# An ordinary first pair in gate and up, and a new end of the down projection, in a layer with two feed-forward halves

## The chip, the cores and the metric

The kernel runs on one core of a Trainium2 chip. The metric is the device time of one execution in microseconds (us). Times in this document are of that kind; TensorE does the matrix products, VectorE and ScalarE the elementwise work, GpSimd a third share of it, and the transfers of this kernel are issued by SyncE.

## The reference

One layer over x of 1024 x 1024 float32, in three residual parts: a feed-forward half, a token mixer, and a second feed-forward half.

```
def swiglu_ffn(x, w_gu, w_down):
    gu = x @ w_gu                       # 1024 x 5632
    g, u = jnp.split(gu, 2, axis=-1)    # gate and up, 2816 each
    return (jax.nn.silu(g) * u) @ w_down
...
x = layer_norm(ALPHA * x + 0.5 * swiglu_ffn(x, ffn1_w_gu, ffn1_w_down), ln1_g, ln1_b)
x = layer_norm(ALPHA * x + hybrid_mixer(x, ...), ln2_g, ln2_b)
x = layer_norm(ALPHA * x + 0.5 * swiglu_ffn(x, ffn2_w_gu, ffn2_w_down), ln3_g, ln3_b)
```

The mixer is gated linear attention and a sparse attention beside each other, with one projection before and one after.

## The kernel before

x is cut into eight blocks of 128 rows; each block has two halves of 512 columns. The feature axis of 2816 has 22 tiles of 128, taken in 11 pairs (`g`). Every matrix product is done in split precision: each operand is split into a high and a low part (`split`, ScalarE L92 for the high part, VectorE L93 for the low one), and a product of two tiles is three matmuls: high by high, high by low, low by high.

Gate and up are done with a scheme of seven block products in place of eight (Strassen's in Winograd's form). x as a whole is one 2 x 2 matrix of quarters: row blocks 0 to 3 or 4 to 7 times left or right half. The quarters "11" and "21" are the two column halves of blocks 0 to 3, "12" and "22" those of blocks 4 to 7; "T1" to "T4" are sums of quarters, and the products use 11, 21, 22 and the four sums. Each of them must first be turned: `turn_in` transposes one half of one block on TensorE in four 128 x 128 pieces into a bank of PSUM (L246, tile `tp`, two banks), and ScalarE and VectorE split it into the tiles `b_h`, `b_l` and the like. The weights' sums are made on GpSimd (L275 to L278) for every pair, for gate and for up (`quad_weights`).

`quad` does the seven products of one pair, of gate or of up. A product is four steps of three matmuls of 128x512 (L300 to L302). In the first pair, the list `self.fill` holds the turns that are still missing, with the sums that they need (L1066 and L1071 on VectorE, L1068 and L1080 on GpSimd); after each step one item of it is popped, so the turns stand between the first products' steps. TensorE takes its instructions in the order in which they were written there (`in_order`). A turn that waits for its x block thus holds the products behind it. In the first half x is loaded from memory at the kernel's start; in the second, blocks 6 and 7 still come out of LayerNorm 2 (L205 to L220) as the first pair begins.

The down projection (`down`) does its seven products `m` = 0 to 6 over 11 steps `i`, each for four row blocks. `prepare` loads a pair of tiles (L410, L411) and splits it into `whid` and `wlod`, in a ring of six; `add` does the matmuls (L420). After a product VectorE adds it into the accumulators and into `u`. In the last product the last five `i` are held back (`ends`), so that its four blocks end one after the other, and each goes through LayerNorm at once (`after_block`). In the first half, `after_all` already turns the blocks 0 to 3 for the mixer between the steps of that last product (`split_T`, TensorE L180, ScalarE L181, VectorE L182). A LayerNorm is two statistics (L205), an aggregate (L207), a small addition (L209), a power on GpSimd (L193), and then either ScalarE L218, GpSimd L219 and VectorE L220, or, for the very last block, VectorE L213 and L214 alone.

Where the order is not written by hand, a planner with costs and due times sets it, in the mixer above all.

Of the kernel before, what the change touches and what calls it, by code (L numbers as in the profile page):

```python
# [111 lines left out]
class Block:  # L112
# [87 lines left out]
    def layer_norm(self, t, g_bc, b_bc, scale=1.0, last=False):  # L200

        nc = self.nc
        st = self.small.tile([P, 2, 6], F32, tag="st", name=self.uid("st"))
        for c in range(2):
            nc.vector.bn_stats(st[:, c, :], t[:, c * 512 : (c + 1) * 512])  # L205
# [6 lines left out]
        if last:  # L212
            nc.vector.scalar_tensor_tensor(t, t, mv[:, 0:1], g_bc, ALU.subtract, ALU.mult)  # L213
            nc.vector.scalar_tensor_tensor(t, t, rs, b_bc, ALU.mult, ALU.add)  # L214
        else:
# [4 lines left out]
            nc.vector.tensor_add(t, t, b_bc)  # L220

# [27 lines left out]
    def feed(self, b, t):  # L249

        if b >= NB // 2:
            self.turn_in(t[:, 512:], b % 4, "22")
        else:
            self.turn_in(t[:, 0:512], b % 4, "11")
            self.turn_in(t[:, 512:], b % 4, "21")

    def quad_raw(self, w_gu, c0):

        r = []
        for k in range(2):  # L260
# [24 lines left out]

    def quad(self, a, weights, ps, cp):
# [6 lines left out]
        def product(left, right):  # L293
            pool, tag, n = ((ps, "y", 2), (ps, "z", 2), (self.ps_pj, "pj", 2))[self.turn % 3]
            self.turn += 1
            bank = pool.tile([P, HT], F32, tag=tag, name=self.uid("pq"), bufs=n)
            wh, wl = a[left]
            xh, xl = self.sums[right]
            for k in range(4):
                nc.tensor.matmul(bank, wh[:, k, :], xh[:, k, :], start=(k == 0), stop=False)  # L300
                nc.tensor.matmul(bank, wh[:, k, :], xl[:, k, :], start=False, stop=False)  # L301
                nc.tensor.matmul(bank, wl[:, k, :], xh[:, k, :], start=False, stop=(k == 3))  # L302
                if self.fill:
                    self.fill.pop(0)()
            return bank

        def tile(name):
            i = self.made_c % sum(n for _, n in cp)
            self.made_c += 1
            pool, n = cp[0] if i < cp[0][1] else cp[1]  # L310
            return pool.tile([P, HT], F32, tag="c", name=self.uid(name), bufs=n)
# [21 lines left out]
    def gate_up(self, w_gu, first, ps, cp, h_dram, w_down, t_dram):  # L333
# [5 lines left out]
        for g in range(NF // 2):  # L339
            if g == 0:  # L340
                both = [self.quad(*w, ps, cp) for w in first]
                for q in both:
                    next(q)
            prods = []
            for i, c0 in enumerate((2 * g * P, FF + 2 * g * P)):
                if g == 0:
                    prods.append(next(both[i]))
                else:
                    a = {}
                    w = self.quad_weights(self.quad_raw(w_gu, c0), a)  # L350
                    next(w)
                    prods.append(list(self.quad(a, w, ps, cp))[-1])
                if i == 0:
                    for t in prods[0]:
                        nc.scalar.activation(t, t, AF.Silu)  # L355
            if g == 0:
                yield
            for t, q in zip(*prods):
                V.tensor_mul(t, t, q)
            (a11, a21, a12, a22), (s1, s2, s4, _) = prods  # L360
            V.tensor_add(s1, a21, a22)
            V.tensor_sub(s2, s1, a11)
            V.tensor_sub(a21, a11, a21)
            V.tensor_sub(s4, a12, s2)
            left = {"A11": a11, "A12": a12, "A22": a22, "S1": s1, "S2": s2, "S3": a21, "S4": s4}
            for m, (name, _) in enumerate(self.DOWN):
                nc.sync.dma_start(h_dram[g][m], left[name])
            if g:
                self.down_sums(w_down, t_dram, g - 1)
        self.down_sums(w_down, t_dram, NF // 2 - 1)  # L370
# [19 lines left out]
    def down(self, w_down, h_dram, t_dram, ps, load, after_block, after_all=None, ordered=None):  # L390
# [33 lines left out]
        ends = range(ng - 5, ng)  # L424
        done = list(range(4))
        acc = None
        for m in range(last + 1):
# [4 lines left out]
            for i in range(ng if m < last else ends[0]):  # L432
# [7 lines left out]
                if m == last and after_all and i >= 2:  # L440
# [3 lines left out]
            for r in range(4):  # L444
# [9 lines left out]
                elif m in (4, 5):  # L454
                    V.tensor_add(u[r], u[r], p)
                else:
# [3 lines left out]
                    after_block(4 + r, acc)  # L460
# [561 lines left out]
    def run(self):  # L1022
# [27 lines left out]
        def first_weights(n, c0):  # L1050

            made = {}
            return made, self.quad_weights(self.quad_raw(a[f"ffn{n}_w_gu"][0], c0), made)

        def front(n, first, blocks, held, left, ps, fed):
# [9 lines left out]
            def t1(b):  # L1065
                V.tensor_sub(t(b - 4, 0), t(b, 0), t(b - 4, 0))  # L1066
                self.turn_in(t(b - 4, 0), b % 4, "T1")
                G.tensor_sub(t(b, 0), t(b, 1), t(b, 0))  # L1068
# [393 lines left out]
```

## Time and profile before

| | |
|---|---|
| time, median of 3 | 2105.14 us (2104.5 to 2107.29) |
| the profiled execution | 2105.46 us, its span 2103.7 |
| mean granted TensorE clock | 0.968 |
| busy share of the span | TensorE 95%, VectorE 73%, ScalarE 40%, GpSimd 30% |
| matmuls of the products in the down projections (L420) | 1848, 34% of the span |

The span runs from the first to the last instruction. Busy shares are averages over parts with different limits, so the stretches at the two starts and ends have to be read by themselves. The granted clock is TensorE's, as a share of 2.4 GHz; 0.5 is its lower level of 1.2 GHz.

### The profile page before, as it was taken

The page shows a single profiled execution, that of the slowest core. Times are in us where ns is not written, and L with a number is a line of the kernel's source. Part 1 is how long each engine was busy: PE and PEld are TensorE (multiplying, and loading weights), DVE is VectorE, ACT ScalarE, POOL GpSimd, SP SyncE. Part 2 cuts the span into 40 slices and gives each one's busy share as a digit, 9 for nine tenths or more (in the row PEclk, how much of TensorE's full clock was granted, in tenths as well). Part 3 has the DMA queues.
Part 4 walks back from the last instruction along what each step waited for, and adds up shares of the span by engine and source line. Part 5 has one row for each costly group of instructions (what it writes and reads, how often), then busy time and mean ns, then how long its engine had stood idle before and what let it go on. Part 6 is the DMA issues. An engine that isn't in the chain of part 4 may idle for free.

```text
span 2103.7 us, 26810 instructions
## 1 busy us (share of the span) xinstructions
PE 1995.0 (95%) x9672; PEld 1618.0 (77%) x9672; DVE 1532.3 (73%) x2398; ACT 849.1 (40%) x1345; POOL 625.5 (30%) x462
## 2 busy tenths in 40 slices
PE   6999999999998899888999999997999999999997
PEld 4888888888887688676777677785888888888885
DVE  7778787785578489998856455558678787775578
ACT  4332323334344344678444344424332323334342
POOL 4345454430012101133233000036444454430022
PEclk9999999999999999899998799999999999999998
DMA  4345445478665132011226621142345445477653
GB/s 155 120 141 185 141 159 181 140 251 286 200 191 166 60 95 86 11 56 51 56 75 156 159 77 36 61 159 84 118 146 183 141 153 178 141 267 277 200 191 140
DMA packets 190982, 298.43 MB, mean 142 GB/s; under 512 B 16113, under 2 KB 98177, under 8 KB 190849
## 3 DMA queue, kind: packets, MB, share of 16 engines
q1 hardware_dynamic: 190848, 296.72, 43.3%
q8 instruction: 76, 1.25, 0.2%
q14 instruction: 58, 0.47, 0.1%
HBM read 205.96 MB, written 90.70 MB: 141 GB/s over the span
## 4 chain that ended last, share of the span: by engine, by line
PE 72%; DVE 14%; issue 6%; DMA 4%; ACT 2%; POOL 1%; SPq 0%; DVEq 0%; ACTq 0%; POOLq 0%
PE pd L420 15%; PE pq L301 12%; PE pq L302 12%; PE pq L300 12%; PE pv L1005 3%; DVE junk L675 2%; PE pt L563 2%; PE pt L564 2%; PE tpe L993 2%; PE pt L565 2%; PE pf L550 2%; PE pf L551 2%; PE pf L552 2%; DVE score L632 1%; DMA rd<-in_ffn_w_down_dram 1%
## 5 line engine op out<-in xcount | busy, mean ns | idle before, releaser
L93 DVE TENSOR_TENSOR wloq<-rw,whiq 128x512 fp32r<-128x512 f32 (+1 forms) x220 | 218.1, 995 | 114.2 <-ACT whiq L92 113.3
L93 DVE TENSOR_TENSOR wlod<-rd,whid 128x1024 fp32r<-128x1024 f32 x154 | 191.6, 1250 | 134.7 <-ACT whid L92 133.4
L92 ACT ACTIVATE whid<-rd 128x1024 fp32r<-128x1024 f32 x154 | 162.9, 1061 | 246.4 <-PE pd L420 155.5
L92 ACT ACTIVATE whiq<-rw 128x512 fp32r<-128x512 f32 (+1 forms) x220 | 170.5, 796 | 219.1 <-POOL rw L278 103.5
L420 PE MATMUL pd<-wlod,whid 128*128 128x512 f32 x616 | 240.5, 391 | 0.1
L420 PE MATMUL pd<-whid,wlod 128*128 128x512 f32 x616 | 240.0, 390 | 0.0
L420 PE MATMUL pd<-whid 128*128 128x512 f32 x616 | 235.9, 392 | 0.0
L300 PE MATMUL pq<-b_h,whiq 128*128 128x512 f32 x528 | 210.4, 398 | 0.0
L301 PE MATMUL pq<-b_l,whiq 128*128 128x512 f32 x528 | 206.8, 392 | 0.3 <-DVE b_l L93 0.3
L302 PE MATMUL pq<-b_h,wloq 128*128 128x512 f32 x528 | 206.8, 392 | 0.0
L275 POOL TENSOR_TENSOR rw<-rw,rw 128x512 f32<-128x512 f32 x44 | 67.8, 1540 | 439.1 <-DVE wloq L93 439.1
L355 ACT ACTIVATE c<-c 128x512 f32<-128x512 f32 x88 | 55.8, 634 | 271.8 <-DVE c L316 182.4
L193 POOL TENSOR_TENSOR rs<-ve,neghalf 128x1 f32<-128x1 f32 x24 | 21.1, 881 | 400.5 <-DVE ve L209 396.7
L300 PE MATMUL pq<-xh,whiq 128*128 128x512 f32 x352 | 137.2, 390 | 0.0
L302 PE MATMUL pq<-xh,wloq 128*128 128x512 f32 x352 | 137.0, 389 | 0.0
L301 PE MATMUL pq<-xl,whiq 128*128 128x512 f32 x352 | 136.9, 389 | 0.0
L563 PE MATMUL pt<-whi,xh 128*128 128x512 f32 x320 | 129.6, 406 | 7.2 <-ACT gg L1266 6.2
L420 PEld LDWEIGHTS pd<-wlod,whid 128*128 128x128 f32 x616 | 116.1, 188 | 25.0 <-DVE wlod L93 1.0
L420 PEld LDWEIGHTS pd<-whid 128*128 128x128 f32 x616 | 116.0, 189 | 25.0 <-ACT whid L92 1.1
L420 PEld LDWEIGHTS pd<-whid,wlod 128*128 128x128 f32 x616 | 116.0, 188 | 24.2
L564 PE MATMUL pt<-wlo,xh 128*128 128x512 f32 x320 | 127.8, 400 | 0.0
L565 PE MATMUL pt<-whi,xl 128*128 128x512 f32 x320 | 127.5, 399 | 0.0
(254 smaller groups left out, 4718.9 us busy)
## 6 DMA issues: line engine op xcount, KB each, us to landing
rw<-in_ffn_w_gu_dram SPq DMA_DIRECT2D x88, 512.0 KB, 4.2
h_dram<-c SPq DMA_DIRECT2D x154, 256.0 KB, 3.0
rd<-h_dram SPq DMA_DIRECT2D x154, 256.0 KB, 3.1
rt<-in_ffn_w_down_dram SPq DMA_DIRECT2D x44, 512.0 KB, 3.8
t_dram<-rt SPq DMA_DIRECT2D x44, 512.0 KB, 3.0
rd<-t_dram SPq DMA_DIRECT2D x88, 256.0 KB, 3.1
rd<-in_ffn_w_down_dram SPq DMA_DIRECT2D x66, 256.0 KB, 4.3
raw<-in_w_in_dram SPq DMA_DIRECT2D x20, 512.0 KB, 3.8
```

What stands on the lines that cost most here:

```text
L92: self.nc.scalar.activation(hi, src, AF.Copy)
L93: self.nc.vector.tensor_sub(lo, src, hi)
L275: G.tensor_add(a22, a21, a22)
L300: nc.tensor.matmul(bank, wh[:, k, :], xh[:, k, :], start=(k == 0), stop=False)
L301: nc.tensor.matmul(bank, wh[:, k, :], xl[:, k, :], start=False, stop=False)
L302: nc.tensor.matmul(bank, wl[:, k, :], xh[:, k, :], start=False, stop=(k == 3))
L355: nc.scalar.activation(t, t, AF.Silu)
L420: nc.tensor.matmul(banks[r], left, right, start=(i == 0 and n == 0), stop=(i == ng - 1 and n == 2))
L563: nc.tensor.matmul(pt, xh[:, k, cols], wh[:, k % 2, :], start=(k == 0), stop=False)
L564: nc.tensor.matmul(pt, xh[:, k, cols], wl[:, k % 2, :], start=False, stop=False)
L565: nc.tensor.matmul(pt, xl[:, k, cols], wh[:, k % 2, :], start=False, stop=(k == KD - 1))
L1005: nc.tensor.matmul(po[j * 64 : j * 64 + 64, q, :], v, ets[j][:, i, :], start=(kb == 0), stop=(kb == b))
```

## The change

The first pair of gate and up, in both halves, is done as eight ordinary block products each, straight from the quarters 11, 12, 21 and 22 with the plain weights (`plain_weights`), so that no weight sums are made for it. The quarter "12" is now turned too, into what later holds T4. The sums T1 to T4 are made while the ordinary products run, and T4 during the first seven-product quad, that of pair 1, which is begun early (`begun`). The turns are no longer popped one after each step but at a step number of their own (`spread`). At the kernel's start, x blocks 0 to 3 are loaded in halves, first halves first, each followed by a half of gate's weights.

In the down projection the last product holds back four `i` in the first half and six in the second; `after_all` starts one `i` later. `c22` and `c21` take `u` already after product 4; product 5 goes straight into both, in place of through `u`, and the statistics of the finished half of blocks 4 to 7 are made there (`stats`). In the second half's LayerNorm the blocks 4 to 7 all take the form that was the last block's, its last instruction in two halves, and each block goes out in two transfers.

```diff
     def layer_norm(self, t, g_bc, b_bc, scale=1.0, last=False, st=None):
...
         if last:
             nc.vector.scalar_tensor_tensor(t, t, mv[:, 0:1], g_bc, ALU.subtract, ALU.mult)
-            nc.vector.scalar_tensor_tensor(t, t, rs, b_bc, ALU.mult, ALU.add)
+            for c in range(2):
+                cs = slice(c * 512, (c + 1) * 512)
+                nc.vector.scalar_tensor_tensor(t[:, cs], t[:, cs], rs, b_bc[:, cs], ALU.mult, ALU.add)
...
+    def plain_weights(self, r):
+
+        out = {}
+        for k, t in enumerate(r, 1):
+            hl = [q.rearrange("p (k f) -> p k f", k=4) for q in self.w.pair(self.uid("q"))]
+            self.w.split(hl, t)
+            for f in range(2):
+                out[f"A{f + 1}{k}"] = [q[:, :, f * P : (f + 1) * P] for q in hl]
+        return out
...
+    def product(self, bank, left, right, start=True, stop=True):
...
+        for k in range(4):
+            mm(bank, wh[:, k, :], xh[:, k, :], start=(start and k == 0), stop=False)
+            mm(bank, wh[:, k, :], xl[:, k, :], start=False, stop=False)
+            mm(bank, wl[:, k, :], xh[:, k, :], start=False, stop=(stop and k == 3))
+            self.step += 1
+            while self.fill and self.fill[0][0] <= self.step:
+                self.fill.pop(0)[1]()
...
+        for c in "12":
+            for i, a in enumerate(first):
+                banks = [self.bank(ps) for _ in range(2)]
+                for k in "12":
+                    for f in range(2):
+                        self.product(banks[f], a[f"A{f + 1}{k}"], k + c, start=(k == "1"), stop=(k == "2"))
+                for f in range(2):
+                    if i == 0:
+                        t = h[f, c] = self.c_tile(cp, "c")
+                        nc.scalar.activation(t, banks[f], AF.Silu)
+                    else:
+                        V.tensor_mul(h[f, c], h[f, c], banks[f])
+        fill(fills[1])
+        begun = quad(1, 0)
+        next(begun)
...
-        ends = range(ng - 5, ng)
+        ends = range(ng - (4 if ordered else RING), ng)
...
-                if m == last and after_all and i >= 2:
+                if m == last and after_all and i >= 3:
                     after_all(done.pop(0), acc)
...
-                elif m in (4, 5):
+                elif m == 4:
                     V.tensor_add(u[r], u[r], p)
+                    V.tensor_add(c12[r], c12[r], u[r])
+                elif m == 5:
+                    V.tensor_add(c22[r], c22[r], p)
+                    V.tensor_add(c21[r], c21[r], p)
...
             elif m == 4:
                 for r in range(4):
-                    V.tensor_add(c12[r], c12[r], u[r])
                     after_block(r, acc)
-            elif m == 5:
-                for r in range(4):
                     V.tensor_add(c22[r], c22[r], u[r])
                     V.scalar_tensor_tensor(c21[r], c21[r], 2.0 * ALPHA, u[r], ALU.mult, ALU.add)
+            elif m == 5:
+                stats = []
+                for r in range(4):
+                    stats.append(self.small.tile([P, 2, 6], F32, tag="st2", name=self.uid("st"), bufs=4))
+                    V.bn_stats(stats[r][:, 1, :], c22[r])
...
+            plain = [(j, name) for j in range(4) if j + 4 not in fed for name in ("12", "22")]
+            pairs = [[(j, name) for name in ("T3", "T2")] for j in range(4)]
+            soon = [item for j in range(len(fed)) for item in pairs[j]]
+            later = [item for j in range(len(fed), 4) for item in pairs[j]] + [(j, "T1") for j in range(4)]
+            rest = soon + plain
+            fills = (
+                spread(2, 2, early) + spread(32 - int(2.75 * len(rest)), 2.75, rest) + spread(34, 27 / len(later), later),
+                spread(2, 2, [(j, "T4") for j in range(4)]),
+            )
...
+            for c in range(2):
+                for b in firsts:
+                    cs = slice(c * 512, (c + 1) * 512)
+                    nc.sync.dma_start(xin[b][:, cs], x[0, b * P : (b + 1) * P, cs])
+                raw += self.quad_raw(w_gu, 0, (c,))
+            raw = [raw, self.quad_raw(w_gu, FF)]
+            for b in seconds:
                 nc.sync.dma_start(xin[b], x[0, b * P : (b + 1) * P, :])
...
-                self.layer_norm(acc[b], *ln, scale=0.5, last=(b == NB - 1))
-                nc.sync.dma_start(out[0, b * P : (b + 1) * P, :], acc[b])
+                self.layer_norm(acc[b], *ln, scale=0.5, last=(b >= 4), st=st)
+                for c in range(2):
+                    cs = slice(c * 512, (c + 1) * 512)
+                    nc.sync.dma_start(out[0, b * P : (b + 1) * P, cs], acc[b][:, cs])
```

The order on TensorE at the start of the second half, of the kernel before. `x2_5` and `x2_6` are blocks 5 and 6 after LayerNorm 2, `b2` the turned quarter, `pq` a product's bank:

```order
L246 MATMUL tp_1914_12091<-ident_72,x2_5_11641 128x128 x4
L300 MATMUL pq_1920_12119<-b2_h_11693,whiq_1853_11679 128x512
L301 MATMUL pq_1920_12119<-b2_l_11694,whiq_1853_11679 128x512
L302 MATMUL pq_1920_12119<-b2_h_11693,wloq_1853_11680 128x512
L246 MATMUL tp_1921_12123<-ident_72,x2_6_11642 128x128 x4
L300 MATMUL pq_1920_12119<-b2_h_11693,whiq_1853_11679 128x512
```

The same place of the changed kernel. Between the first row of `pq` and the turn of `x2_4` lie ten steps, of which the first and the last are shown; between that turn and the one of `x2_6` eleven more, with three turns of blocks 4 and 5:

```order
L251 MATMUL tp_1909_12106<-ident_72,x2_5_11655 128x128 x4
L305 MATMUL pq_1914_12127<-b2_h_11694,whiq_1846_11686 128x512
L306 MATMUL pq_1914_12127<-b2_l_11695,whiq_1846_11686 128x512
L307 MATMUL pq_1914_12127<-b2_h_11694,wloq_1846_11687 128x512
...
L307 MATMUL pq_1914_12127<-b2_h_11694,wloq_1847_11691 128x512
L251 MATMUL tp_1916_12163<-ident_72,x2_4_11654 128x128 x4
...
L251 MATMUL tp_1923_12218<-ident_72,x2_5_11655 128x128 x4
...
L307 MATMUL pq_1922_12211<-b2_h_11694,wloq_1912_12117 128x512
L251 MATMUL tp_1924_12234<-ident_72,x2_6_11656 128x128 x4
```

Block 6 moved from behind the first step to behind the twenty-first.

The order on VectorE at the end of the first half, of the kernel before: `pd` is product 5 in its bank, `u1` the accumulator u, `wlod` a weight's low half, and `xl` the first low half that the mixer takes:

```order
L220 TENSOR_TENSOR acc1_3_3694<-acc1_3_3694,b_bc_446_3709 128x1024
L93 TENSOR_TENSOR wlod_626_5115<-rd_625_5111,whid_626_5114 128x1024
L455 TENSOR_TENSOR u1_0_3711<-u1_0_3711,pd_587_4811 128x512
...
L470 TENSOR_TENSOR acc1_4_3695<-acc1_4_3695,u1_0_3711 128x512
L471 SCALAR_TENSOR_TENSOR acc1_4_3695<-acc1_4_3695,u1_0_3711 128x512
...
L205 BN_STATS st_647_5261<-acc1_4_3695 128x6
...
L93 TENSOR_TENSOR wlod_642_5228<-rd_641_5224,whid_642_5227 128x1024
L182 TENSOR_TENSOR xl_432_3618<-tp_623_5097,xh_431_3617 128x4x128
```

And of the changed kernel:

```order
L224 TENSOR_TENSOR acc1_1_3695<-acc1_1_3695,b_bc_439_3712 128x1024
L509 TENSOR_TENSOR acc1_4_3698<-acc1_4_3698,pd_580_4822 128x512
L510 TENSOR_TENSOR acc1_4_3698<-acc1_4_3698,pd_580_4822 128x512
...
L528 BN_STATS st_606_5043<-acc1_4_3698 128x6
L224 TENSOR_TENSOR acc1_2_3696<-acc1_2_3696,b_bc_439_3712 128x1024
...
L224 TENSOR_TENSOR acc1_3_3697<-acc1_3_3697,b_bc_439_3712 128x1024
...
L93 TENSOR_TENSOR wlod_641_5262<-rd_640_5258,whid_641_5261 128x1024
L182 TENSOR_TENSOR xl_425_3621<-tp_622_5131,xh_424_3620 128x4x128
```

Each block's product is added twice here (L509, L510), each has a statistic (L528), and the norms of blocks 2 and 3 (L224) stand behind the first additions; the additions of u moved ahead of this piece.

The order on VectorE at the very end, of the kernel before (block 7's addition and what follows):

```order
L459 TENSOR_TENSOR acc2_7_15495<-acc2_7_15495,pd_2506_16836 128x512
L205 BN_STATS st_2544_17095<-acc2_7_15495 128x6
L220 TENSOR_TENSOR acc2_5_15493<-acc2_5_15493,b_bc_2336_15506 128x1024
L207 BN_AGGR mv_2545_17098<-st_2544_17095 128x2
L217 SCALAR_TENSOR_TENSOR nb_2543_17073<-mv_2540_17067,rs_2542_17071 128x1
L209 TENSOR_SCALAR ve_2546_17100<-mv_2545_17098 128x1
L213 SCALAR_TENSOR_TENSOR acc2_7_15495<-acc2_7_15495,mv_2545_17098,g_bc_2335_15504 128x1024
L214 SCALAR_TENSOR_TENSOR acc2_7_15495<-acc2_7_15495,rs_2547_17102,b_bc_2336_15506 128x1024
L220 TENSOR_TENSOR acc2_6_15494<-acc2_6_15494,b_bc_2336_15506 128x1024
```

And of the changed kernel, from block 7's addition on:

```order
L514 TENSOR_TENSOR acc2_7_15501<-acc2_7_15501,pd_2496_16858 128x512
L218 SCALAR_TENSOR_TENSOR acc2_5_15499<-acc2_5_15499,rs_2524_17051,b_bc_2322_15512 128x512 x2
L209 BN_AGGR mv_2525_17078<-st_2491_16851 128x2
L207 BN_STATS st_2492_16853<-acc2_7_15501 128x6
L211 TENSOR_SCALAR ve_2526_17080<-mv_2525_17078 128x1
L215 SCALAR_TENSOR_TENSOR acc2_6_15500<-acc2_6_15500,mv_2525_17078,g_bc_2321_15510 128x1024
L209 BN_AGGR mv_2528_17109<-st_2492_16853 128x2
L218 SCALAR_TENSOR_TENSOR acc2_6_15500<-acc2_6_15500,rs_2527_17082,b_bc_2322_15512 128x512 x2
L211 TENSOR_SCALAR ve_2529_17111<-mv_2528_17109 128x1
L215 SCALAR_TENSOR_TENSOR acc2_7_15501<-acc2_7_15501,mv_2528_17109,g_bc_2321_15510 128x1024
L218 SCALAR_TENSOR_TENSOR acc2_7_15501<-acc2_7_15501,rs_2530_17113,b_bc_2322_15512 128x512 x2
```

VectorE now does the whole LayerNorm of blocks 5, 6 and 7 but for the power.

## Rows read from the trace of the kernel before

**Rows 1.** The page: the chain that ended last, by engine, and a costly group.

```profile
PE 72%; DVE 14%; issue 6%; DMA 4%; ACT 2%; POOL 1%; SPq 0%; DVEq 0%; ACTq 0%; POOLq 0%
...
L93 DVE TENSOR_TENSOR wlod<-rd,whid 128x1024 fp32r<-128x1024 f32 x154 | 191.6, 1250 | 134.7 <-ACT whid L92 133.4
```

**Rows 2.** The chain in order of time: start us, us, what.

```profile
1906.37 175.11 PE pd L420 x770
```

**Rows 3.** Timeline of TensorE (PE), start of the first half: start us, us, instruction, idle.

```profile
15.02 0.47 PE L300 MATMUL pq<-b_h,whiq 128*128 128x512 f32 x1
...
22.59 1.09 PE L246 MATMUL tp<-ident,xin 128*128 128x128 f32 x4 [3.74 <-issue]
...
41.21 0.47 PE L300 MATMUL pq<-b_h,whiq 128*128 128x512 f32 x1
...
42.34 0.48 PE L300 MATMUL pq<-b_h,whiq 128*128 128x512 f32 x1
```

**Rows 4.** Windows of the tile pq, both starts: the products' matmuls are PE's count.

```profile
0.00:57.00 57.00, 23.13 (x69) 12.65 (x70) 1.37 (x2) 1.78 (x3) 0.91 0.43 152
1432.40:1475.00 42.60, 22.41 (x71) 13.06 (x72) 1.37 (x2) 1.79 (x3) 0.88 0.24 81
```

**Rows 5.** Windows of the tile tp, both starts: the transposes are PE's count.

```profile
0.00:57.00 57.00, 21.20 (x112) 16.13 (x112) 18.89 (x28) 16.45 (x28) 0.91 0.43 152
1432.40:1475.00 42.60, 12.78 (x75) 9.21 (x73) 12.93 (x19) 11.28 (x19) 0.88 0.24 81
```

**Rows 6.** Timeline of ScalarE (ACT), its first instructions.

```profile
5.53 1.28 ACT L92 ACT_TABLE_LOAD   x1 [5.53 <-PE tp L246]
6.82 1.09 ACT L92 ACTIVATE b_h<-tp 128x512 fp32r<-128x512 f32 x2
```

**Rows 7.** Windows of all engines, start of the first half (columns in the first row).

```profile
core 0: us, PE busy (x) PEld busy (x) DVE busy (x) ACT busy (x) POOL busy (x), PEclk, DMA share, GB/s
...
10.00:15.00 5.00, 2.99 (x17) 1.96 (x17) 4.31 (x7) 3.27 (x6) 2.89 (x3) 1.00 1.03 410
...
20.00:25.00 5.00, 2.37 (x7) 1.58 (x7) 5.00 (x5) 1.29 (x3) 4.70 (x3) 0.70 0.00 0
25.00:30.00 5.00, 3.81 (x14) 2.96 (x14) 5.00 (x9) 3.81 (x6) 1.07 (x1) 0.62 0.00 2
```

**Rows 8.** The same view, start of the second half and end of the first.

```profile
1430.00:1440.00 10.00, 3.36 (x17) 2.45 (x15) 10.00 (x11) 4.02 (x5) 8.52 (x5) 0.93 0.35 116
1440.00:1450.00 10.00, 6.75 (x26) 5.52 (x27) 8.14 (x10) 2.94 (x5) 9.10 (x7) 0.56 0.25 94
...
640.00:650.00 10.00, 10.00 (x50) 8.38 (x49) 10.00 (x14) 2.37 (x3) 0.00 (x0) 1.00 0.90 314
```

**Rows 9.** Timelines of TensorE and VectorE (DVE), start of the second half.

```profile
1443.25 1.08 PE L246 MATMUL tp<-ident,x 128*128 128x128 f32 x4 [9.90 <-DVE mv L207]
...
1441.43 1.68 DVE L220 TENSOR_TENSOR x<-x,b_bc 128x1024 f32<-128x1024 f32 x1
...
1451.56 1.21 DVE L220 TENSOR_TENSOR x<-x,b_bc 128x1024 f32<-128x1024 f32 x1
```

**Rows 10.** Timeline of TensorE behind the first half.

```profile
657.98 1.97 PE L180 MATMUL tp<-ident,acc 128*128 128x128 f32 x8 [5.41 <-DVE xl L182]
...
702.92 0.69 PE L625 MATMUL ps<-ik_hi,iq 128*128 128x384 f32 x1 [9.33 <-DVE iq L595]
```

**Rows 11.** Timelines of VectorE and GpSimd (POOL), the tail.

```profile
2079.24 0.69 DVE L459 TENSOR_TENSOR acc<-acc,pd 128x512 f32<-128x512 f32 x1 [0.94 <-PE pd L420]
2079.96 1.29 DVE L205 BATCH_NORM_STATS2 st<-acc 128x6 f32<-128x512 f32 x2
...
2087.37 3.37 DVE L220 TENSOR_TENSOR acc<-acc,b_bc 128x1024 f32<-128x1024 f32 x1 [0.17 <-POOL acc L219]
...
2095.14 3.35 DVE L214 SCALAR_TENSOR_TENSOR acc<-acc,rs,b_bc 128x1024 f32<-128x1024 f32 x1 [0.44 <-POOL rs L193]
2098.41 1.21 DVE L220 TENSOR_TENSOR acc<-acc,b_bc 128x1024 f32<-128x1024 f32 x1
...
2093.64 1.46 POOL L193 TENSOR_TENSOR rs<-ve,neghalf 128x1 f32<-128x1 f32 x1 [2.49 <-DVE ve L209]
```

More of the change, by code (lines that the diff above doesn't have):

```diff
@@ L198, in bcast_row, with layer_norm @@
         return t
-    def layer_norm(self, t, g_bc, b_bc, scale=1.0, last=False):
+    def layer_norm(self, t, g_bc, b_bc, scale=1.0, last=False, st=None):
         nc = self.nc
-        st = self.small.tile([P, 2, 6], F32, tag="st", name=self.uid("st"))
-        for c in range(2):
+        made = st is not None
+        if not made:
+            st = self.small.tile([P, 2, 6], F32, tag="st", name=self.uid("st"))
+        for c in range(1 if made else 2):
             nc.vector.bn_stats(st[:, c, :], t[:, c * 512 : (c + 1) * 512])
@@ L284, in quad_weights, with bank, c_tile @@
             self.w.split(hl, t)
+    def product(self, bank, left, right, start=True, stop=True):
+        wh, wl = left
+        xh, xl = self.sums[right]
+        mm = self.nc.tensor.matmul
+        for k in range(4):
[5 more added lines that the diff above has]
+                self.fill.pop(0)[1]()
+    def bank(self, ps):
+        pool, tag, n = ((ps, "y", 2), (ps, "z", 2), (self.ps_pj, "pj", 2))[self.turn % 3]
+        self.turn += 1
+        return pool.tile([P, HT], F32, tag=tag, name=self.uid("pq"), bufs=n)
+    def c_tile(self, cp, name):
+        i = self.made_c % sum(n for _, n in cp)
+        self.made_c += 1
+        pool, n = cp[0] if i < cp[0][1] else cp[1]
+        return pool.tile([P, HT], F32, tag="c", name=self.uid(name), bufs=n)
     def quad(self, a, weights, ps, cp):
@@ L293, in product @@
         def product(left, right):
[L294 to L304, printed above, removed]
+            bank = self.bank(ps)
+            self.product(bank, a[left], right)
             return bank
         def tile(name):
[L308 to L311, printed above, removed]
+            return self.c_tile(cp, name)
         c21 = tile("c21")
@@ L331, in quad, with gate_up, fill, store @@
         yield c11, c12, c21, c22
-    def gate_up(self, w_gu, first, ps, cp, h_dram, w_down, t_dram):
+    def gate_up(self, w_gu, first, fills, ps, cp, h_dram, w_down, t_dram):
         nc = self.nc
         V = nc.vector
[L339 to L361, printed above, removed]
+        def fill(items):
+            assert not self.fill
+            self.step = 0
+            self.fill = list(items)
+        def quad(g, i):
+            a = {}
+            w = self.quad_weights(self.quad_raw(w_gu, i * FF + 2 * g * P), a)
+            next(w)
+            return self.quad(a, w, ps, cp)
+        def store(g, h, spare):
+            a11, a12, a21, a22 = h
+            s1, s2, s4 = spare
+            V.tensor_add(s1, a12, a22)
             V.tensor_sub(s2, s1, a11)
-            V.tensor_sub(a21, a11, a21)
-            V.tensor_sub(s4, a12, s2)
-            left = {"A11": a11, "A12": a12, "A22": a22, "S1": s1, "S2": s2, "S3": a21, "S4": s4}
+            V.tensor_sub(a12, a11, a12)
+            V.tensor_sub(s4, a21, s2)
+            left = {"A11": a11, "A12": a21, "A22": a22, "S1": s1, "S2": s2, "S3": a12, "S4": s4}
             for m, (name, _) in enumerate(self.DOWN):
@@ L1048, in run, with front @@
         firsts, seconds = range(NB // 2), range(NB // 2, NB)
[L1050 to L1055, printed above, removed]
+        def front(n, first, blocks, held, left, ps, early, fed):
             V, G = nc.vector, nc.gpsimd
@@ L1089, in front, with spread @@
+            def spread(at, gap, items):
+                return [(at + int(gap * i), turned(*item)) for i, item in enumerate(items)]
             cp = [(left.enter_context(tc.tile_pool(name=f"early{n}", bufs=1, reuse_waits="tile")), 6)]
             self.made_c = 0
[L1091 to L1098 removed]
+            self.sums["T4"] = self.sums["12"]
@@ L1130, in two_pools @@
             held, tiles = [], {}
-            for which, bs in (("second", seconds), ("first", firsts)):
+            for which, bs in (("first", firsts), ("second", seconds)):
                 held.append(ExitStack())
```

113 lines of the change are left out of this document (56 added, 57 removed).

## The prediction

> **What bounds the kernel now.** I read the chain first, by engine: TensorE holds 72% of it, VectorE 14% [rows 1]. So the sum is made in TensorE time: what work is added to it, and which of its idle stretches go. Its price stands in the chain in order of time: 770 matmuls of 128x512 in 175.11 us, 0.2274 us each [rows 2]. A turn (four 128x128 transposes, one block of x) goes between two steps of three matmuls that start 1.13 us apart, so it costs 1.13 − 3 × 0.2274 = 0.45 us [rows 3].
>
> Next, the two starts of the feed-forward halves, by counts. In the first 57 us TensorE did 69 such matmuls and 112 transposes (28 turns) [rows 4, 5]: 15.7 + 12.6 = 28.3 us of work at full clock, so 28.7 us are idle or slow. 11.4 of it lies ahead of the first product at 15.02 (eight turns, 3.6 us, are done by then); ScalarE only begins at 5.53, with a table load of 1.28 [rows 3, 6]. Behind it 17.3 remain: a wait of 3.74 at 22.59, shorter ones, and a granted clock of 0.70 and 0.62 from 20 to 30 us, where VectorE is busy 5.00 of 5 [rows 3, 7]. At the start of the second half, from 1432.4 to 1475 (42.6 us), the counts are 71 matmuls and 75 transposes (a record may be missing), 16.1 + 8.4 = 24.5 us of work, so 18.1 idle: after three matmuls TensorE stands 9.90 us for the LayerNorm of block 6, whose turn comes behind the first step, and then the clock is 0.56 for 10 us [rows 4, 5, 8, 9].
>
> Last, two places where VectorE is the bound: the end of the first half (10.00 of 10 us at 640 to 650; TensorE then stands 5.41 us at 657.98 for the first low half of an x block, L182) [rows 8, 10], and the tail, where VectorE ends at 2099.6 [rows 11].
>
> **The change, part by part.** *The first pair, added work.* Sixteen block products of 12 matmuls replace fourteen: 24 × 0.2274 = 5.45 us; four blocks more are turned ("12"): 1.8. That is 7.25 us a half, 14.5 in all, none of it hidden, since TensorE is the bound once it runs. In return GpSimd makes no weight sums for the first pair.
>
> *Start of the first half.* The first product needs four turned blocks instead of eight. On ScalarE: 6.81 after the table load, four high halves at 0.55 (two take 1.09) [rows 6], one high half of a weight, about 1.1: 10.1; its low half on VectorE takes 1.25 [rows 1] and ends at 11.3. I take 10.7 for the first product: 10.7 − 4 × 0.45 = 8.9 idle ahead of it, instead of 11.4. Behind it the block sums are no longer wanted within the first products, but from step 34 on, a step being three matmuls. Blocks 4 to 7 are wanted at step 10, some 10.7 + 6.8 + 1.8 = 19.3 us, and the loads have ended by 20 [rows 7]; VectorE takes its work in order behind them: I put 3 us there, and 1.6, a tenth of what is there now, for smaller waits. Idle 13.5, so the gain is 28.7 − 13.5 − 7.25 = 8.0. Bounds: the first product stays at 15.02, and half of the idle behind it: 28.7 − 11.4 − 8.7 − 7.25 = 1.4; no wait behind the first product: 28.7 − 8.9 − 7.25 = 12.6. I take a value nearer the upper one because VectorE gets 32 low halves and 16 subtractions or products of 0.65 and four weight splits of 1.25, some 36 us, for 64 steps (44 us) and their turns (12): on the whole it is ahead.
>
> *Start of the second half.* By the order, 30 matmuls run before the first turn that can wait (block 4), and block 6 comes at step 21, not at 1. From 1432.4, 21 steps (14.3 us) and four turns (1.8) reach 1448.5; block 6's LayerNorm ended at 1443.1 and block 7's at 1452.8, which step 26 wants at about the same time [rows 9]. GpSimd, which takes part in these LayerNorms and is 8.52 and 9.10 of 10 us busy there [rows 8], loses four sums. Of the 18.1 idle, 8.2 would be left if the 9.90 alone went; the slow clock that follows it is part of these. I leave 3.3 us. Gain 18.1 − 3.3 − 7.25 = 7.55. Bounds: 8.2 stay: 2.65; nothing stays: 10.85.
>
> *End of the first half.* Between product 4 and the first L182, VectorE's order holds seven more halves of 0.65 (eight additions of the product in place of four, three statistics more) and one more weight split of 1.25: 5.8 us. The norms of blocks 0 to 3 are neither more nor fewer. TensorE has one more i of the last product ahead of its wait (12 matmuls, 2.7 us). Loss 5.8 − 2.7 = 3.1. Bounds: the statistics made early are saved later, and the wait of 9.33 at 702.92, which also ends with VectorE, takes up the rest [rows 10]: −1; nothing of the 5.8 is covered: +5.8.
>
> *Tail.* By the order the last product ends blocks 4 and 5 interleaved, so block 4 is whole some 2.3 us later, about 2081.5 instead of 2079.2 (ten matmuls). From then VectorE does for each of four blocks an addition and one statistic at 0.65, 0.2 of small instructions, 1.21 for the subtraction and 1.21 in two halves: 3.9, 15.7 in all, and 0.6 of waiting for GpSimd's power. 2081.5 + 15.7 + 0.6 = 2097.8, against 2099.6. Gain 1.8; that the last transfer is half as large I count at nothing. Bounds 0 (a power waits in full for each block) and 4 (the interleaving costs nothing). What goes is GpSimd's multiplication: today L220 takes 3.37 and L214 3.35 where it runs beside them, and 1.21 without [rows 11].
>
> *Rule and row.* L214 is some 2.1 us longer beside GpSimd's work, and the power takes 1.46 where VectorE has a two-input instruction of its own running [rows 11]. The Trainium skill (SBUF — State Buffer, "Who interferes with whom") says that VectorE and GpSimd share a port pair, and that the first to start blocks the other for its whole instruction. By the row the sum stands as above; by the rule a power that starts first also holds VectorE, four times in the tail.
>
> *The mixer* between the halves is planned anew and its instructions come in another order; the arithmetic is the same. I take 0, and ± 4 as bounds, somewhat under half of its first wait of 9.33 either way [rows 10].
>
> **Sum.** −8.0 − 7.55 + 3.1 − 1.8 + 0 = −14.25. The profiled execution took 2105.46 (its span and 1.76 around it), 0.3 above the median of 2105.14. 2105.46 − 14.25 = 2091.2.
>
> **Rivals.** *VectorE is the real bound of both starts (slower).* Then the waits only move: TensorE's idle stays, and 14.5 us come on top: 2105.46 + 14.5 + 3.1 − 1.8 = 2121.3. For it: VectorE's 5.00 of 5 and 10.00 of 10 [rows 7, 8]. Against: the long wait of the second half has a single cause, one turn wanted too early. It decides when more than 46.8 − 14.5 − 3.1 + 1.8 = 31.0 of the 46.8 idle us stay.
>
> *Loads set the start of the first half.* The queue already moves 410 GB/s from 10 to 15 us [rows 7], and x now comes in more and smaller pieces among the weights. The first product stays near 15, blocks 4 to 7 come late, the clock falls again: a gain of 2 there instead of 8: 2097.2. The Trainium skill (DMA: Bandwidth & Descriptors, "Measured (HBM→SBUF, 128 partitions, SWDGE, issued from GpSimd)") asks for transfers of at least 1 MiB and so speaks against the halves; no row here separates that from the queue's order.
>
> *VectorE's debt at the end of the first half is paid in full*: 5.8 instead of 3.1, and a mixer that is planned 3 us worse: 2096.9.
>
> *The lock in the tail*: a power that starts first, at its 1.46, stops VectorE for four blocks: 4 × 1.46 − 0.6 = 5.2 us, and the tail loses 3.4 instead of gaining 1.8: 2096.4.
>
> **Chances.** The forecast 0.55, with a range of its own of 2084 to 2097 (the bounds of the two starts are not met together); loads 0.20; debt 0.11; lock 0.05; VectorE the bound 0.09. A comparison of this kernel can tell about 0.2% (4.2 us) from no change. Faster: 0.54 + 0.18 + 0.10 + 0.04 = 0.86; slower, from VectorE the bound with most of the idle kept, 0.07; the same takes the rest, 0.07. The range runs over the loads, debt and lock cases to their far side by the mixer's bound, and below to where both starts come nearer their upper bounds: 2081 to 2102.
>
> **What would show it.** Right: a first product near 10.7 and no wait over 2 us between there and 57; a granted clock near 1.00 from 20 to 30; no wait of 9.90 behind 1420; a longer stand than 5.41 for L182 near 645; in the tail no GpSimd multiplication for blocks 4 to 7 and no VectorE instruction above 2 us. Wrong: waits for VectorE's low halves from step 10 on that add up to more than 15 us a half; a first product that stays at 15; or a mixer whose stretch from the end of the first half to LN2 is over 4 us longer.

## The result and the profile after

The changed kernel takes 2081.19 us (median of 4, 2077.77 to 2082.8), the kernel before 2105.7 beside it: a ratio of 0.9879 (95% interval 0.9867 to 0.9892). 2091.2 with a range of 2081 to 2102 had been forecast. The profiled execution took 2082.8 with a span of 2081.0, 22.7 less than before.

The two starts went nearly as written. The counts of [rows 4, 5], in the changed kernel (windows of the tile pq, then of tp; the second stretch is as long as the one shown of before and begins with the first product):

```profile
0.00:57.00 57.00, 39.35 (x142) 26.01 (x143) 1.38 (x2) 1.79 (x3) 1.00 0.49 166
...
1418.10:1460.70 42.60, 37.42 (x144) 26.81 (x145) 1.38 (x2) 1.69 (x3) 0.96 0.22 75
```

```profile
0.00:57.00 57.00, 15.59 (x92) 12.79 (x92) 14.80 (x22) 12.87 (x22) 1.00 0.49 166
...
1418.10:1460.70 42.60, 8.56 (x55) 6.68 (x52) 9.50 (x14) 8.47 (x15) 0.96 0.22 75
```

In 42.6 us TensorE now does 144 matmuls and some 14 turns, 32.7 + 6.2 = 38.9 us of work: 3.7 idle, where 18.1 were and 3.3 had been written. In the first 57 us it does 142 and 23 turns, 42.6 us of work: 14.4 idle, where 28.7 were and 13.5 had been written. The clock is 1.00 throughout, where [rows 7] had 0.70 and 0.62, and VectorE, 5.00 of 5 in both rows there, is at 3.81 and 4.83 (columns as in [rows 7]):

```profile
20.00:25.00 5.00, 3.70 (x19) 2.40 (x18) 3.81 (x7) 1.73 (x3) 0.00 (x0) 1.00 1.08 351
25.00:30.00 5.00, 5.00 (x28) 4.13 (x27) 4.83 (x5) 4.09 (x7) 3.02 (x3) 1.00 0.26 81
```

The timeline of TensorE gives the first product at 10.91 (10.7 was written), one wait of 1.97 at the second start, where 9.90 stood, and at the end of the first half the wait for L182, 7.72 in place of 5.41 [rows 3, 9, 10]:

```profile
10.91 0.80 PE L305 MATMUL pq<-b_h,whiq 128*128 128x512 f32 x1 [1.42 <-ACT b_h L92]
...
1427.13 0.63 PE L251 MATMUL tp<-ident,x 128*128 128x128 f32 x4 [1.97 <-DVE xl L93]
...
656.47 1.97 PE L180 MATMUL tp<-ident,acc 128*128 128x128 f32 x8 [7.72 <-DVE xl L182]
```

In the tail (timelines of VectorE and GpSimd) no single instruction of VectorE takes above 1.28 (the 1.41 are of two halves), and it stands 0.44 for the last power, which still takes 1.46 [rows 11]:

```profile
2074.70 1.28 DVE L215 SCALAR_TENSOR_TENSOR acc<-acc,mv,g_bc 128x1024 f32<-128x1024 f32 x1
2076.42 1.41 DVE L218 SCALAR_TENSOR_TENSOR acc<-acc,rs,b_bc 128x512 f32<-128x512 f32 x2 [0.44 <-POOL rs L193]
...
2074.93 1.46 POOL L193 TENSOR_TENSOR rs<-ve,neghalf 128x1 f32<-128x1 f32 x1 [1.66 <-DVE ve L211]
```

The surprise lies between the halves. The table cuts the spans at the first matmul of a kind: the first of the down projection; the first of its last product; the mixer's first projection (tile pf); the first and the middle one of tile pt, between which most of the linear attention runs beside the key search; the attention's first pv; the first product of the second half; and so on to the end. The column of before is in us, all others are differences from it, each from one profile:

| stretch | before | after | front_only | front_form | ends5 | x_whole | six_early | tail_old | down_only | form_only | first_ends6 |
|---|---|---|---|---|---|---|---|---|---|---|---|
| start of first half | 460.43 | −6.76 | −5.92 | −6.74 | −6.64 | −2.64 | −6.45 | −6.74 | +2.43 | +3.30 | +0.58 |
| down, six products | 180.17 | +0.22 | −0.19 | −0.24 | −0.30 | +0.45 | +0.21 | −0.03 | +0.53 | −0.40 | −0.15 |
| last product to mixer | 41.89 | +1.57 | −0.23 | −0.77 | +2.39 | +1.03 | +2.70 | +0.71 | +2.11 | −0.71 | −0.30 |
| index scores | 164.74 | −1.53 | −0.07 | −0.41 | −0.91 | −1.45 | −1.06 | −1.66 | −1.21 | −0.38 | −3.22 |
| attention and search | 210.90 | −10.88 | −9.85 | −9.79 | −2.21 | −2.80 | −8.45 | −11.81 | −2.31 | −0.29 | −6.05 |
| to the first pv | 123.54 | +0.74 | +2.11 | −2.37 | −2.42 | +2.03 | −0.81 | −2.11 | +1.78 | 0.00 | −0.67 |
| first pv to second half | 250.75 | +2.31 | +2.34 | +2.37 | +2.42 | +1.51 | +2.13 | +2.22 | +1.24 | −0.03 | +1.06 |
| start of second half | 445.46 | −7.62 | −7.61 | −7.56 | −7.59 | −7.55 | +7.76 | −7.56 | +0.01 | 0.00 | 0.00 |
| down, six products | 180.05 | +0.39 | +0.61 | +1.42 | +0.27 | +0.67 | +0.49 | +0.43 | +1.11 | −0.53 | +1.24 |
| last product to the end | 45.76 | −1.11 | −0.25 | −2.64 | −0.75 | −0.97 | −0.24 | +2.35 | +0.84 | −2.67 | −0.28 |
| span | 2103.68 | −22.67 | −19.07 | −26.72 | −15.75 | −9.72 | −3.72 | −24.20 | +6.53 | −1.70 | −7.79 |

The mixer (the four rows from the index scores to the second half) is 9.36 us shorter, and 10.88 of it lies where search and linear attention share VectorE. Without it the change is worth 22.67 − 9.36 = 13.3, against 14.25 written.

### The profile page after: what moved, and what is told of

It is laid out like the page before. It is cut to its first block, busy times and chain, and to the rows that moved or that the text cites. A ratio compares the mean times of both kernels' runs of the same rounds, so it can differ in the third digit from the quotient of the medians.

```text
span 2081.0 us, 26915 instructions
## 1 busy us (share of the span) xinstructions
PE 2004.6 (96%) x9752; PEld 1627.6 (78%) x9752; DVE 1500.3 (72%) x2378; ACT 836.1 (40%) x1330; POOL 591.6 (28%) x443
## 4 chain that ended last, share of the span: by engine, by line
PE 73%; DVE 16%; issue 4%; DMA 3%; ACT 2%; POOL 1%; SPq 0%; POOLq 0%; DVEq 0%; ACTq 0%
PE pq L305 13%; PE pq L307 13%; PE pq L306 13%; PE pd L471 13%; DVE junk L732 3%; PE pv L1062 3%; PE tpe L1050 2%; PE pf L607 2%; PE pf L608 2%; DVE wlod L93 2%; PE pf L609 2%; PE pt L620 2%; PE pt L622 1%; PE pt L621 1%; DVE score L689 1%
## 5 line engine op out<-in xcount | busy, mean ns | idle before, releaser
L93 DVE TENSOR_TENSOR wloq<-rw,whiq 128x512 fp32r<-128x512 f32 (+1 forms) x208 | 213.8, 1030 | 110.9 <-ACT whiq L92 110.4
L93 DVE TENSOR_TENSOR wlod<-rd,whid 128x1024 fp32r<-128x1024 f32 x154 | 189.2, 1235 | 132.4 <-ACT whid L92 131.4
L92 ACT ACTIVATE whiq<-rw 128x512 fp32r<-128x512 f32 (+1 forms) x208 | 163.5, 806 | 224.9 <-POOL rw L291 93.4
L305 PE MATMUL pq<-b_h,whiq 128*128 128x512 f32 x576 | 229.2, 398 | 2.1 <-ACT b_h L92 2.1
L306 PE MATMUL pq<-b_l,whiq 128*128 128x512 f32 x576 | 225.7, 392 | 1.2 <-DVE b_l L93 1.2
L307 PE MATMUL pq<-b_h,wloq 128*128 128x512 f32 x576 | 225.6, 392 | 0.0
L417 ACT ACTIVATE c<-c 128x512 f32<-128x512 f32 x80 | 50.5, 632 | 238.8 <-DVE c L341 156.1
L305 PEld LDWEIGHTS pq<-b_h,whiq 128*128 128x128 f32 x576 | 108.9, 189 | 23.8 <-ACT b_h L92 2.7
```

What stands on the lines that cost most here:

```text
L92: self.nc.scalar.activation(hi, src, AF.Copy)
L93: self.nc.vector.tensor_sub(lo, src, hi)
L305: mm(bank, wh[:, k, :], xh[:, k, :], start=(start and k == 0), stop=False)
L306: mm(bank, wh[:, k, :], xl[:, k, :], start=False, stop=False)
L307: mm(bank, wl[:, k, :], xh[:, k, :], start=False, stop=(stop and k == 3))
```

## The experiments

**front_only**: the changed kernel with the old functions at the end of `down` and in LayerNorm.

```diff
-        ends = range(ng - (4 if ordered else RING), ng)
+        ends = range(ng - 5, ng)
...
-                elif m == 5:
-                    V.tensor_add(c22[r], c22[r], p)
-                    V.tensor_add(c21[r], c21[r], p)
+                elif m in (4, 5):
+                    V.tensor_add(u[r], u[r], p)
```

> The changed kernel with the old end of the down projection, the old LayerNorm and the old tail: only the first pairs and their turns are changed. Both theories: start of the first half 6.8 us earlier than before, start of the second half 7.6 us, the end of the first half and the tail as before (0 +- 0.5). Theory A (the mixer's 9.35 us come from the order in which the planner lets VectorE alternate between the key search and the gated linear attention; this kernel has an order of its own): the mixer's time is different from before, by a size that the theory does not give (say -5 +- 8); total 2081 to 2097. Theory B (the mixer gains because the new end of the down projection hands it its first blocks in another rhythm): the mixer as before, 0 +- 1; total 2105.5 - 14.4 = 2091.

2081.21 us, ratio 0.989 (0.9872 to 0.9908), as fast as the whole change. The starts give −5.9 and −7.6, the ends −0.2 each, the attention −9.85 and the mixer as a whole −5.5: it doesn't need the new end of the down projection to gain (theory B fell).

**down_only**: the kernel before with the new end alone (the reverse of the above).

> The kernel before with the new end of the down projection, the new statistics and the new tail: the first pairs are as before. Both theories: end of the first half +1.7 us, tail -1.1. Theory A: VectorE's order in search and attention is that of the kernel before but for the very end, so the mixer is as before, 0 +- 1; total 2105.5 + 0.6 = 2106. Theory B: the mixer's 9.35 us come with it; total 2096.7.

2109.84 us, ratio 1.0019 (1.001 to 1.0028): slower, by little. The first half's end costs 2.1 (1.7 expected), the attention is −2.31, the mixer as a whole −0.5: theory A's number, not B's. The tail missed: 1.1 shorter was expected, 0.84 longer came. The +2.43 at the first start, which this edit does not touch, is spread of the old start (see below).

**tail_old**: the changed kernel with `last=(b == NB - 1)` in `norm2`.

> The changed kernel, but in the second half's last LayerNorm blocks 4 to 6 take the old form (ScalarE, GpSimd, VectorE) and only block 7 the new one. By the prediction's tail term (GpSimd's multiplication stretches VectorE's instructions from 1.21 to 3.4 us): the tail 2 to 4 us longer than in the changed kernel, 2084. If the new form is worth nothing: the same as the changed kernel, 2081.2. The mixer's order is that of the changed kernel, so theory A and theory B both say the changed kernel's mixer, within 1 us.

2084.02 us, ratio 0.9897 (0.9882 to 0.9913). The tail is 3.5 us longer than in the changed kernel (+2.35 against −1.11). The order in the mixer is that of the changed kernel row for row, on all engines, and the attention is again as short (−11.81). That the stretch from there to the first pv came out 2.9 us shorter at the same order is part of what stays open below.

**six_early**: block 6 turned first again at the start of the second half.

```diff
-            rest = soon + plain
+            rest = plain + soon if fed else soon + plain
...
-                spread(2, 2, early) + spread(32 - int(2.75 * len(rest)), 2.75, rest) + spread(34, 27 / len(later), later),
+                spread(2, 2, early) + spread(1 if fed else 32 - int(2.75 * len(rest)), 2.75, rest) + spread(34, 27 / len(later), later),
```

> The changed kernel, but at the start of the second half the turns begin at step 1 and block 6's come first, then those of block 7, then the sums of blocks 4 and 5: the place of the turns of before with the ordinary products of the change. If the gain of the second half's start comes from block 6 being wanted late: a wait of 8 to 10 us for its LayerNorm is back within the first steps, that start 5 to 9 us longer than in the changed kernel. If it came from the ordinary products themselves (less work on GpSimd and VectorE ahead of the LayerNorms): not over 3 us longer. Its mixer has an order of its own, so the total says less than the stretch: theory A lets the mixer differ, theory B says the changed kernel's mixer within 1 us.

2098.47 us, ratio 0.9959 (0.9942 to 0.9975). That start is 15.4 us longer than in the changed kernel, where 5 to 9 had been expected. Its two waits (timeline of TensorE) are for blocks 6 and 7:

```profile
1432.47 1.09 PE L251 MATMUL tp<-ident,x 128*128 128x128 f32 x4 [10.83 <-DVE mv L209]
1443.54 0.63 PE L251 MATMUL tp<-ident,x 128*128 128x128 f32 x4 [4.06 <-DVE x L224]
```

So the whole gain of that start, and the 7.25 us of added work that it pays for, hangs on the place of the turns. An order of its own had been expected in the mixer; it is the changed kernel's, row for row on all engines, and the attention is −8.45.

**first_ends6**: the kernel before with one number changed.

```diff
-        ends = range(ng - 5, ng)
+        ends = range(ng - (RING if ordered else 5), ng)
```

> The kernel before with one number changed: in the first half the last product holds back six i instead of five. No first pair, no sums, no tail is touched. The planner then gives VectorE another order of search and attention in the mixer (about as far from before as the changed kernel's is). Theory A (the mixer's gain is a matter of that order alone): the mixer differs from before by more than 2 us, most likely by -4 to -10, the first half's end by 0 +- 2, all else 0; total 2097 to 2103. Theory C (the mixer's gain needs the new first pairs, which both kernels with it had, and the order is a bystander): the mixer as before, 0 +- 1; total 2105 +- 2.

2098.6 us, ratio 0.9967 (0.9953 to 0.998). No start, no sum and no tail is touched, and every stretch but the mixer is within 1.3 us of before; the mixer is 8.89 shorter. This is the run that settles theory A against theory C: another order in the mixer, without the change, is enough for a gain of nearly the same size (6.05 of it in the attention, 3.22 in the index scores).

**front_form**: front_only with the new form of the last LayerNorm, in halves; **form_only**: that form alone on the kernel before.

```diff
-                self.layer_norm(acc[b], *ln, scale=0.5, last=(b == NB - 1))
-                nc.sync.dma_start(out[0, b * P : (b + 1) * P, :], acc[b])
+                self.layer_norm(acc[b], *ln, scale=0.5, last=(b >= 4))
+                for c in range(2):
+                    cs = slice(c * 512, (c + 1) * 512)
+                    nc.sync.dma_start(out[0, b * P : (b + 1) * P, cs], acc[b][:, cs])
```

> The new first pairs with the old end of the down projection, and of the new end only the form of the second half's last LayerNorm (blocks 4 to 7 on VectorE alone, in halves, two transfers each). If the form's worth (3.5 us between the changed kernel and the one with the old form) does not need the new ends: the tail 3 to 4 us shorter than before, total 2081.2 - 3.5 = 2077.7, faster than both kernels. If it needs the blocks that end interleaved: the tail as before, 2081.

> The kernel before with only the new form of the last LayerNorm in blocks 4 to 7 (its last instruction and the output in halves). VectorE's order in the mixer is that of before, row for row. Theory A: the stretch of the linear attention as before (0 +- 2.5, the size by which the kernel with only the new end differed there); the tail 2.6 us shorter, as with the new first pairs; total 2105.5 - 2.6 = 2103. If a kernel's mixer moves from profile to profile by as much as 10 us at the same order: any attention stretch between 200 and 211.

front_form: 2083.79 us, ratio 0.9892 (0.9873 to 0.9911), with the shortest profile of the eleven (2077.0) and a median that can't be told from the changed kernel's; the 2077.7 expected of it, faster than both kernels, is missed. form_only: 2103.9, ratio 0.9991 (0.9981 to 1.0). In both the tail is 2.65 us shorter, so the form's worth needs neither the new ends nor the first pairs. form_only's order in the mixer is that of before, and its attention differs by 0.29.

**x_whole**: the changed kernel with x loaded in whole blocks.

```diff
-            for c in range(2):
-                for b in firsts:
-                    cs = slice(c * 512, (c + 1) * 512)
-                    nc.sync.dma_start(xin[b][:, cs], x[0, b * P : (b + 1) * P, cs])
-                raw += self.quad_raw(w_gu, 0, (c,))
+            for b in range(NB):
+                nc.sync.dma_start(xin[b], x[0, b * P : (b + 1) * P, :])
+                if b == 1:
+                    raw[0] = self.quad_raw(w_gu, 0)
```

> The changed kernel with x loaded in whole blocks in the old order (blocks 0 and 1, gate's weights, blocks 2 to 7, up's weights). If the halves bring the first product forward: first product near 13 to 15 us instead of 10.9, the start of the first half 2 to 4 us longer than in the changed kernel. By the rule that larger transfers are better: no longer, or shorter. The mixer's order is its own again: theory A -4 to -10 against before.

2094.95 us, ratio 0.9946 (0.9928 to 0.9963). The first product stands at 13.21 instead of 10.91, and the start loses 4.1 of its 6.8 us. Whole blocks in this order do not pay here; size and order of the transfers changed together, so neither is shown alone. Its mixer as a whole is only −0.7 (the attention −2.8): theory A's guess of −4 to −10 missed, as an order of its own can also be a poor one.

```profile
13.21 0.79 PE L305 MATMUL pq<-b_h,whiq 128*128 128x512 f32 x1 [0.69 <-ACT b_h L92]
```

**ends5**: the changed kernel with five `i` held back in both halves and the turns one step earlier (`i >= 2`).

> The changed kernel with five i held back in both halves, as before, and the turns of blocks 0 to 3 one step earlier. Debt of additions (eight product additions in place of four ahead of L182): the first half's end stays 1.5 to 2.5 us longer than before. Debt of the ends: it is as before, 0 +- 0.5. In the tail: if six held back i cost what the tail lost (2.4 us with the old form), the tail is 3 to 4 us shorter than before; if not, 1 us shorter as in the changed kernel.

2090.19 us, ratio 0.9924 (0.9909 to 0.994). The first half's end stays 2.39 longer than before, with this wait, so the debt is that of the additions and statistics and not of the number held back. In the tail too the number makes no difference to speak of: TensorE ends 32.5 us after the last product began, as in the changed kernel (30.3 before), and the stretch is −0.75.

```profile
654.32 1.97 PE L180 MATMUL tp<-ident,acc 128*128 128x128 f32 x8 [8.69 <-DVE xl L182]
```

This kernel has the change's parts but for the number held back and that step, an attention of only −2.21, and a time 1 us from the forecast.

**short_before, short_after**: both kernels with 8 of the search's 31 rounds.

```diff
-        for p in range(30, -1, -1):
+        for p in range(30, 22, -1):
```

> The kernel before with 8 of the 31 rounds of the key search; the other 23 are left out, so fewer keys are told apart, and the search takes a quarter of its work on VectorE and ScalarE. To be compared with the same cut of the changed kernel, in the stretch of the linear attention (from the first matmul of the gates' projection, tile pt, to its middle one; 210.9 us before, 200.0 in the changed kernel). Theory A, sharpened (the 10.9 us lie in how the search is dealt out among the attention's steps): with little search left the two stretches differ by less than 3 us. Rival D (TensorE's own order of projections and attention steps makes them): they still differ by 8 us or more.

> The changed kernel with 8 of the 31 rounds of the key search, the other 23 left out. See the same cut of the kernel before: theory A, sharpened: the stretch of the attention within 3 us of that one's; rival D: shorter by 8 us or more.

2089.86 and 2073.59 us, one run each. The stretch of attention and search, as windows (columns as in [rows 7]), of before, after, short_before and short_after:

```profile
847.20:1058.10 210.90, 182.49 (x943) 144.26 (x942) 195.92 (x546) 144.95 (x276) 55.29 (x42) 0.91 0.15 43
```

```profile
840.70:1040.80 200.10, 181.74 (x944) 143.36 (x943) 191.15 (x536) 144.61 (x276) 53.68 (x42) 0.92 0.16 45
```

```profile
850.50:1044.50 194.00, 177.49 (x938) 141.73 (x937) 126.32 (x231) 92.52 (x179) 58.12 (x41) 0.93 0.16 48
```

```profile
841.10:1034.80 193.70, 178.40 (x938) 142.35 (x937) 123.09 (x231) 92.53 (x179) 58.72 (x41) 0.92 0.16 48
```

With a quarter of the search, both kernels need 194.0 and 193.7 us: 10.8 us of difference became 0.3, so it needs the search. The full search costs the kernel before 16.9 us there and the changed one 6.4. Rival D is not out by this, though: the two short kernels have the same order in this stretch on TensorE and on every other engine, while the full ones differ on TensorE as well (some 230 of its 942 instructions there stand elsewhere). What is shown is that the orders to which the search leads make the difference, not that VectorE's alone does.

VectorE is busy 195.92 of 210.9 (15.0 idle) and 191.15 of 200.1 (9.0 idle). The 4.8 us less of work are mostly moved, not saved: the changed order puts eleven VectorE instructions fewer into this stretch, and as many more into the next, where VectorE is busy about half of the time (they are of the selection that ends the search, tile `keep`). Of the 6.0 us less idle, 4.3 is one wait, in which VectorE's small search instruction stands for ScalarE's part of the search (groups by line of the two stretches; the last column is idle before, and for what):

```profile
L677 DVE TENSOR_SCALAR search<-search 128x1 int32<-128x1 f32 x64 | 9.6, 151 | 9.4 <-ACT junk L672 9.1
```

```profile
L734 DVE TENSOR_SCALAR search<-search 128x1 int32<-128x1 f32 x64 | 9.5, 149 | 5.1 <-ACT junk L729 4.9
```

TensorE feels this directly. Its waits in the two stretches that the trace puts down to VectorE's search instructions, which are the last that VectorE ended before TensorE went on, before and after (us in total, times, longest):

```profile
PE pd L849 <- DVE search L677: 7.1, 1, 7.1
PE pa L877 <- DVE search L677: 5.5, 2, 5.0
PE pa L877 <- DVE search L689: 4.8, 1, 4.8
```

```profile
PE po L960 <- DVE search L746: 2.6, 1, 2.6
PE pa L934 <- DVE search L734: 1.8, 2, 1.0
PE pa L934 <- DVE search L736: 0.7, 1, 0.7
PE po L960 <- DVE search L734: 0.3, 1, 0.3
```

17.4 us became 5.4, and all of TensorE's waits there 27.8 and 18.0: 9.8 of the 10.8 us. The kernels fall into groups by the order of this stretch, the same in a group on all engines, but for two VectorE instructions in down_only and for at most eight of an engine between ends5 and x_whole (us; "stage" is ScalarE's copy of a projection out of its bank):

| order | the stretch | TensorE waits, search | TensorE waits, stage | VectorE's small search instruction waits |
|---|---|---|---|---|
| before, form_only, down_only | 210.9, 210.6, 208.6 | 17.4 to 17.5 | 0 | 9.2 to 10.0 |
| ends5, x_whole | 208.7, 208.1 | 7.7 | 8.3 | 10.4, 9.7 |
| first_ends6 | 204.9 | 7.5 | 5.9 | 7.5 |
| front_only, front_form | 201.1, 201.1 | 1.9, 2.3 | 2.2, 2.4 | 5.8, 5.7 |
| after, six_early, tail_old | 200.1, 202.5, 199.1 | 4.5 to 5.4 | 1.7 to 2.0 | 5.1 to 6.0 |

Within a group the stretch differs by up to 3.4 us, over all eleven kernels by 12.

## Why the prediction was wrong

The step that failed is the mixer's: "planned anew ... I take 0, and ± 4 as bounds, somewhat under half of its first wait of 9.33 either way". It measured −9.36. The bound came from a wait of TensorE in another stretch, the index scores, which moved by −1.53. The right rows would have been those of the stretch of attention and search, where VectorE is busy 93% of 211 us and TensorE waits 17.4 us behind its search instructions: a new order moves these waits. Over these eleven kernels that stretch is 199 to 211 us. The prediction's sign of being wrong was a mixer over 4 us longer; a shorter one was not looked for. That the time came out at the lower end of the range is no merit of it: that end was kept for starts near their upper bounds, and neither start came near its own.

The other steps, against the table; their misses, of up to 1.5 us, go both ways, so that 13.3 lies near 14.25 partly by luck:
- Start of the first half, −8.0: −6.76 in this profile. The five profiles of kernels with the old start and load order (short_before's is +3.71) lie at 0 to +3.7, so against their mean of 2.0 the gain is nearer 8.8. First product and clock were right; the loads case (a gain of 2) nearly came true in x_whole, which is the change without its halves.
- Start of the second half, −7.55: −7.62, and six_early shows the cause.
- End of the first half, +3.1: +1.57 in the profile; the five profiles with the same new end of this half lie at +0.71 to +2.70, with a mean of 1.6 (ends5, one step earlier, +2.39). The wait for L182 grew by 2.3. The reason was right; the term was about twice too large.
- Tail, −1.8: −1.11. The form is worth 2.65 alone; the new end takes the rest. TensorE's last matmul of the tail is 2.2 us later after the last product's begin than before, 1.1 of it in two waits for weights (`wlod`, VectorE L93) that it did not have before.
- The lock: the power takes 1.46 four times, as in [rows 11], and VectorE waits 0.32 and 0.44 for two of them. Each time VectorE's L215 had begun 0.23 us earlier (2074.70 and 2074.93 in the last), so the rival's condition, a power that starts first, did not occur.
- VectorE as the bound of both starts is out: 14.3 and 14.4 us of idle went, not moved.

Not shown: which part of the change gave the planner its new order. front_only and first_ends6 change different things, and both reorder. Nor is it shown which engine's order counts for how much: the planner moved TensorE's, VectorE's and ScalarE's together. Not settled either: the stretch from the attention's middle to the first pv, which came out at +0.74 and −2.11 (after, tail_old), or +2.11 and −2.37 (front_only, front_form), at the same order on all engines. The granted clock differs there (0.84 and 0.90 over that stretch of front_only and front_form, 0.50 and 0.68 in a 15 us window of it), but whether that is cause or effect was not tried. Executions of one kernel lie 5 to 8 us apart in several of these runs; this stretch, and the old start's 3.7 us, may be part of why.

## What to carry to other kernels

Where a planner orders the work, a change anywhere ahead can reorder a stretch in which one engine is nearly full; compare the orders there, bound the term by that stretch's spread under small edits (12 us here, against the ± 4 that were written), and judge a change by its own stretches before its total. At the second start the order was worth more than the work: turns that come 20 steps later were worth 15 us, more than the 7 us that the ordinary products cost.

## What the runs showed that had not been expected

One number in the end of the first half, with no gain of its own, made the kernel before 0.33% faster through the mixer (first_ends6). And the new end of the down projection, which belongs to a change that gains 1.2%, makes the kernel 0.19% slower by itself.
